# A two-layer hybrid decoder trunk on one core: norm factor broadcast a step later, first gate ahead of its mixing, recurrence gates moved around the output products, block products reordered

## The chip, the cores and the metric

The kernel runs on one core of a Trainium2 chip. The metric is device time in microseconds (us) of one execution; lower is better. A core has a matrix engine (TensorE, PE in the profile; PEld is its weight load), VectorE (DVE), ScalarE (ACT), GpSimd (POOL) and SyncE (SP), each working through its own list of instructions in order, and 16 DMA engines that all queues share. An instruction waits, where it has to, for a semaphore of another engine, and holds up everything behind it in its own list.

## The reference

Input x is 512 tokens by 1024 features; there are two layers. Cut to what matters here:

```python
for i in range(2):
    y = rms_norm(h, mix_norm[i])
    proj = y @ w_in[i]            # 1024 -> 6144, split into nine parts
    x_lru, g_lru, q, k, v, g_ret, u_sgu, v_sgu, g_sgu = split(proj)
    lru = rg_lru(causal_conv(x_lru), ...)            # 768 wide, 8 blocks of 96
    ret = retention(q, k, v, ...)                    # 6 heads of 128
    sgu = u_sgu * (w_s (per 128 tokens) @ layer_norm(v_sgu) + b_s)   # 512 wide
    mixed = concat(lru * silu(g_lru), ret * silu(g_ret), sgu * silu(g_sgu))
    h = h + mixed @ w_out[i]
    z = rms_norm(h, ple_norm[i])
    h = h + sigmoid(z @ w_ple_gate[i]) * (p[i] @ w_ple_proj[i])
return rms_norm(h, final_norm)
```

In rg_lru, two gates of each 96-wide block (sigmoids of small products) set the coefficients of a recurrence along the tokens: h[t] = a[t] h[t-1] + u[t].

## The kernel before, in words

**Number format.** A product is made in three matmuls (`mm3`, L212): every operand is split into a high part in a narrower format (`whi`, `y` with an even number) and the remainder (`wlo`, the odd number), and hi x hi, hi x lo and lo x hi are summed in PSUM. L214, L215 and L216 are these three.

**Weights.** `plan()` (L41) lists all weight chunks of 128 x 1024 in the order of their use. `prefetch` (L174) loads chunk i into a `raw` buffer (four of them) by SP's queue and converts it (`emit_cv`, L151): ACT casts it to `whi` (L165); the remainder is made by DVE (L170) or, for the chunks that L166 names, by ACT writing the negated copy into `wlo` (L167) and GpSimd's queue issuing a DMA that adds the chunk from memory to it (L168). `whi` and `wlo` have four buffers each, so a conversion waits until the chunk four places earlier has been used up on PE. In the first layer L166 names chunks 4 and 5, in the second all six chunks of x_lru (89 to 94 in the list).

**Order.** The code is written in steps (`step`, L192): prefetch up to four chunks ahead, the matmuls, then up to three pieces of background work from `bg` and one from `lazy`, then the evictions. The program's scheduler then merges these into a list for each engine, by its own estimates; the order within a list is fixed from then on.

**A layer.** It starts with six blocks of x_lru: a step of three blocks side by side (accumulators in three of the four PSUM banks `mm`), then three single ones. The norm's factor per token is wanted only after the products (the weights of the norm are folded into y, the factor is multiplied in at the evictions). `norm_stat` (L307) makes it: small matmuls `nst`, a chain of small DVE operations, and two diagonal matrices `nsgm` and `nsq`; `norm_bcast` (L335) spreads it over all partitions as `R` with two matmuls (`nR`, L337 and L338) and an ACT copy. The evictions of the blocks (`conv`, L545) multiply by `R` into `xs`; the taps `xcv` (L550, L552) follow and a DMA on ACT's queue puts the result into `U`.

Then come the products for v (four heads) and v_sgu as a 2 x 2 block product with seven products instead of eight (`FAST`, L30; `fast_step`, L590): W11, W21, Ta, Tc, Tb, Td, W22, each with two chunks and 24 matmuls. The sums of the y side are `uy` (L505 to L522, from ACT's `fz` and DVE's `fe`). The sums of the weight side are made in memory: W11's raw buffer `rawq` gets W12 added by a DMA of GpSimd's queue to become Ta, then W22 to become Tc, then W21 to become Td; each addition has to wait until the conversion before it has read the buffer. Tb is made of two blocks in a buffer of its own.

Next are four column blocks c of the spatial gate, each two steps of 24 matmuls: u with the mixing matmuls `mx` (L715) at its end, then the gate gs (`silu_scaled`); `fin` multiplies and splits into `sm`. The mixing needs the layer norm of v_sgu (`ln_apply`, ended by the four DVE operations of L635). Ahead of blocks 1 and 3 stand the gates of the recurrence groups 0 and 1 (`lru_group`, L645: four gate products of three matmuls each from `xc`, the split of U, then tanh, exp and square root on ACT and the recurrence on DVE, L689 to L693). `sgu_out` (L745) makes the part of the output product that belongs to the spatial gate, four steps f of 24 matmuls from `sm`, with group 2's gates ahead of f = 2; group 3's gates follow. Six heads of retention, the gates of the recurrence part, the rest of the output product and the per-layer embedding follow; the change leaves their order alone.

## Time and profile before

| | us |
|---|---|
| median of three runs | 933.3 |
| lowest and highest | 929.15, 934.02 |
| the profiled execution | 927.7 |
| its span, first to last instruction | 926.0 |
| mean granted TensorE clock (share of full speed) | 0.997 |

A row of the timeline has the start in us, the duration, engine, line and operation, what is written and read, and how many instructions were merged into the row; in brackets stands the idle time just before it and what ended it. Names in a row have their numbers left out. Matmuls overlap: one shows some 0.39 us, while the next begins 0.23 us after it. The profile names the releaser that came last by its events.

### The profile page before, as it was taken

Reading aid. Unit: us, or ns where it says so; the run is one execution under the profiler, and the core shown is the slowest. Engines: PE = TensorE matmul, PEld = TensorE weight load, DVE = VectorE, ACT = ScalarE, POOL = GpSimd, SP = SyncE. Lnnn points to the kernel's source line nnn. Section 1 sums busy time; section 2 is a strip of 40 time slices with the busy share of each in tenths; the row PEclk is TensorE's granted clock in tenths of the full one; section 3 lists DMA queues with packets and bytes.
Section 4 is the critical chain, followed back from the end, with each engine's and each line's share of the span. In section 5 each row is a group of like instructions: output and inputs, shape, how many; then the busy total and the mean of one; then the engine's idle time right before and its main releaser. Section 6 shows DMA issues by size and latency. Waiting matters only on the chain.

```text
span 926.0 us, 11714 instructions
## 1 busy us (share of the span) xinstructions
PE 901.6 (97%) x4354; PEld 748.7 (81%) x4354; DVE 659.7 (71%) x1281; ACT 460.5 (50%) x666; POOL 51.1 (6%) x52
## 2 busy tenths in 40 slices
PE   8999999999999999999989999999999999999997
PEld 7778787788888888888777778778889888888886
DVE  6979998987766754449529798789776676534564
ACT  6655678833233443335627438876333334334353
POOL 0210000000000000100311100000000000011020
PEclk9999999999999999999999999999999999999999
DMA  9968223232223433342558742232222323233302
GB/s 318 216 136 260 80 74 103 87 114 88 73 69 97 119 98 92 119 137 89 137 111 198 171 150 75 74 113 91 93 79 66 106 75 119 86 108 120 109 1 91
DMA packets 35177, 105.14 MB, mean 114 GB/s; under 512 B 4656, under 2 KB 5680, under 8 KB 35120
## 3 DMA queue, kind: packets, MB, share of 16 engines
q1 hardware_dynamic: 27248, 84.64, 28.3%
q0 software_dynamic: 3456, 12.58, 7.5%
q10 hardware_dynamic: 4416, 7.17, 2.6%
q8 instruction: 34, 0.56, 0.3%
q14 instruction: 23, 0.19, 0.1%
HBM read 95.99 MB, written 2.10 MB: 106 GB/s over the span
## 4 chain that ended last, share of the span: by engine, by line
PE 74%; DVE 9%; DMA 7%; ACT 5%; issue 4%; POOL 0%; ACTq 0%; DVEq 0%; POOLq 0%
PE acc L215 22%; PE acc L216 22%; PE acc L214 22%; DMA rawq<-in_wall 3%; DVE wlo L170 3%; DMA wlo<-in_wall 2%; DMA raw<-in_wall 2%; PE sc L824 1%; PE o L847 1%; DVE xcv L552 1%; ACT whi L165 1%; PE o L849 1%; PE kv L835 1%; PE pp L214 1%; DVE U L693 1%
## 5 line engine op out<-in xcount | busy, mean ns | idle before, releaser
L165 ACT CAST whi<-raw 128x1024 fp32r<-128x1024 f32 (+2 forms) x157 | 153.0, 978 | 303.2 <-PE acc L215 225.0
L214 PE MATMUL acc<-y,whi 128*128 128x512 f32 x608 | 242.0, 398 | 2.5 <-ACT whi L473 1.3
L216 PE MATMUL acc<-y,wlo 128*128 128x512 f32 x608 | 238.3, 392 | 3.9 <-DMA wlo<-in_wall 3.3
L215 PE MATMUL acc<-y,whi 128*128 128x512 f32 x608 | 237.8, 391 | 0.0
L170 DVE TENSOR_TENSOR wlo<-raw,whi 128x1024 fp32r<-128x1024 f32 (+2 forms) x149 | 167.4, 1125 | 75.2 <-ACT whi L165 75.0
L216 PEld LDWEIGHTS acc<-y,wlo 128*128 128x128 f32 x608 | 114.4, 188 | 30.0 <-DMA wlo<-in_wall 5.6
L214 PEld LDWEIGHTS acc<-y,whi 128*128 128x128 f32 x608 | 114.7, 189 | 25.9 <-ACT whi L473 1.6
L215 PEld LDWEIGHTS acc<-y,whi 128*128 128x128 f32 x608 | 114.8, 189 | 22.7
L305 POOL TENSOR_TENSOR nacc<-nacc,sq 128x512 f32<-128x512 f32 (+1 forms) x21 | 28.3, 1349 | 492.5 <-ACT sq L295 492.5
L214 PE MATMUL acc<-z,whi 128*128 128x512 f32 (+1 forms) x144 | 53.0, 368 | 0.0
L216 PE MATMUL acc<-z,wlo 128*128 128x512 f32 (+1 forms) x144 | 52.8, 366 | 0.0
L215 PE MATMUL acc<-z,whi 128*128 128x512 f32 (+1 forms) x144 | 52.7, 366 | 0.0
L214 PE MATMUL acc<-whi,y 128*128 128x256 f32 (+1 forms) x112 | 38.1, 341 | 1.2 <-ACT vs L615 1.2
L214 PE MATMUL acc<-ml,whi 128*128 128x512 f32 x96 | 37.3, 389 | 0.0
L215 PE MATMUL acc<-ml,whi 128*128 128x512 f32 x96 | 37.3, 389 | 0.0
L216 PE MATMUL acc<-rm,wlo 128*128 128x512 f32 x96 | 37.3, 389 | 0.0
L214 PE MATMUL acc<-rm,whi 128*128 128x512 f32 x96 | 37.3, 389 | 0.0
L216 PE MATMUL acc<-ml,wlo 128*128 128x512 f32 x96 | 37.3, 389 | 0.0
L215 PE MATMUL acc<-rm,whi 128*128 128x512 f32 x96 | 37.3, 389 | 0.0
L215 PE MATMUL acc<-wlo,y 128*128 128x256 f32 (+1 forms) x112 | 36.8, 329 | 0.0
L216 PE MATMUL acc<-whi,y 128*128 128x256 f32 (+1 forms) x112 | 36.8, 329 | 0.0
L912 DVE TENSOR_TENSOR hT<-hT,acc 128x512 f32<-128x512 f32 x16 | 11.0, 686 | 29.9 <-PE acc L216 29.9
(232 smaller groups left out, 1647.6 us busy)
## 6 DMA issues: line engine op xcount, KB each, us to landing
raw<-in_wall SPq DMA_DIRECT2D x119, 512.0 KB, 3.5
raw<-in_wall SPq DMA_DIRECT2D x32, 384.0 KB, 3.1
rawq<-in_wall POOLq DMA_DIRECT2D x12, 512.0 KB, 7.0
wlo<-in_wall POOLq DMA_DIRECT2D x8, 512.0 KB, 8.3
hT<-in_xT SPq DMA_DIRECT2D x8, 256.0 KB, 4.9
rawq<-in_wall SPq DMA_DIRECT2D x4, 512.0 KB, 5.9
raw<-in_wall POOLq DMA_DIRECT2D x4, 512.0 KB, 9.0
out_dram<-o SPq DMA_DIRECT2D x8, 256.0 KB, 2.1
```

The source lines that it names most:

```text
L165: SC.copy(hi[:m, :n], r[:m, :n])
L170: V.tensor_sub(lo[:m, :n], r[:m, :n], f32(hi[:m, :n]))
L214: T.matmul(out, wh, xh, start=first, stop=False, skip_group_check=more)
L215: T.matmul(out, wh, xl, start=False, stop=False, skip_group_check=more)
L216: T.matmul(out, wl, xh, start=False, stop=last, skip_group_check=more)
L305: (V if d == KD - 1 else e).tensor_add(nrm["acc"][:, c], nrm["acc"][:, c], sq[:, :n])
L552: V.scalar_tensor_tensor(u[:, j:], xs[:, : S - j], col(V_CW, l * 24 + 6 * (3 - j) + c), u[:, j:], op0=ALU.mult, op1=ALU.add)
L693: V.tensor_tensor_scan(u, A, u, 0.0, op0=ALU.mult, op1=ALU.add)
L824: T.matmul(b[:, n, :], k[:, c], q[:, c], start=True, stop=True)
L835: T.matmul(kv[:, n, :], hd["kn"][:, n, :], values(h, n), start=True, stop=True)
L847: T.matmul(o[:, c], hd["s"][:, n, :], values(h, n), start=True, stop=n == 0)
L912: V.tensor_add(hT[:, d, :], hT[:, d, :], accs[j])
```

## The change

1. `FAST`: Ta stands second, ahead of W21 (the plan of chunks follows).
2. `plan()`: in the first column block the gate gs stands ahead of u, and `osg`, the chunks of `sgu_out`, follow group 2's gate weights; the loop over c and `sgu_out` follow: group 2's gates stand ahead of `sgu_out`, and the splits of U for groups 1, 2 and 3 are queued one step later, after the gate step, and in step f = 0.
3. L166: chunks 89, 90 and 91 (the first three of x_lru in the second layer) get their remainder from DVE, no longer from ACT and a DMA.
4. The first half of the first three chunks is loaded by SP's queue, in turn with the pieces of x, no longer by ACT's queue.
5. The evictions of the first three blocks of x_lru are held back until block 3 has been multiplied, `norm_stat` stays with the step of three, and `norm_bcast` comes after block 3; blocks 4 and 5 take their accumulators from the two banks `sc`.
6. `fin` of the first column block is queued by u's eviction.

```diff
--- before.py
+++ after.py
@@ -27,7 +27,7 @@
 LRU_GROUPS = [(0, 1), (2, 3), (4, 5), (6, 7)]
 
 
-FAST = (("W11", "x11", "X"), ("W21", "x12", "Z"), ("Ta", "u1", "Y"), ("Tc", "v2", "X"), ("Tb", "v3", "X"), ("Td", "x22", "X"), ("W22", "u4", "Y"))
+FAST = (("W11", "x11", "X"), ("Ta", "u1", "Y"), ("W21", "x12", "Z"), ("Tc", "v2", "X"), ("Tb", "v3", "X"), ("Td", "x22", "X"), ("W22", "u4", "Y"))
 FIRST = ("W11", "W21", "Ta")
 RSQRT_MAGIC = 1597463007.0
 ROUND = 12582912.0
@@ -48,8 +48,8 @@
         for c in range(4):
             if c % 2 == 1:
                 out += [lg[c // 2]]
-            out += [(l, "in", OFF["u"] + P * c, 1024), (l, "in", OFF["gs"] + P * c, 1024)]
-        out += [(l, "osg", 0, 1024), (l, "osg", 1, 1024), lg[2], (l, "osg", 2, 1024), (l, "osg", 3, 1024), lg[3]]
+            out += [(l, "in", OFF[n] + P * c, 1024) for n in (("u", "gs") if c else ("gs", "u"))]
+        out += [lg[2]] + [(l, "osg", f, 1024) for f in range(4)] + [lg[3]]
         for h in range(NH):
             if h == 4:
                 out += [(l, "inv", (OFF["v"] + P * h, kh), 1024) for kh in range(2)]
@@ -163,7 +163,7 @@
             lo = wp.tile([P, 1024], F32R, tag="wlo", name=f"wlo{i}")
             m = rows(chunks[i])
             SC.copy(hi[:m, :n], r[:m, :n])
-            if kind == "in" and idx < OFF["gl"] and i > 3:
+            if kind == "in" and 3 * P <= idx < OFF["gl"] and i > 3:
                 SC.activation(lo[:m, :n], r[:m, :n], AF.Copy, scale=-1.0)
                 G.dma_start(out=lo[:m, :n], in_=source(chunks[i]), accum_op=ALU.add)
             else:
@@ -229,12 +229,11 @@
 
     first3 = [wp.tile([P, 1024], F32, tag="raw", name=f"raw{i}") for i in range(3)]
     half = [slice(0, 512), slice(512, 1024)]
-    for i in range(3):
-        nc.scalar.dma_start(out=first3[i][:, half[0]], in_=source(chunks[i])[:, half[0]])
     for d in range(KD):
         nc.sync.dma_start(out=hT[:, d, :], in_=a["xT"][:, d, :])
-        if 3 <= d < 6:
-            nc.sync.dma_start(out=first3[d - 3][:, half[1]], in_=source(chunks[d - 3])[:, half[1]])
+        if d < 6:
+            i, h = d % 3, half[d // 3]
+            nc.sync.dma_start(out=first3[i][:, h], in_=source(chunks[i])[:, h])
     st.update(raw=3, cv=3)
     spt = tp.tile([P, S], F32, tag="r0", name="spt")
     lam, *sp_tmp = [spt[:, 2 * NB * i : 2 * NB * i + 2 * NB] for i in range(5)]
@@ -344,14 +343,14 @@
         nrm["rn"] = rn
 
 
-    def feat_steps(l, y, kinds, evicts, look=LOOK, n_bg=3, mid=None, n_lazy=1):
+    def feat_steps(l, y, kinds, evicts, look=LOOK, n_bg=3, mid=None, n_lazy=1, tag=()):
 
         accs = []
 
         def pe():
             ws = [take(l, *k) for k in kinds]
             for _ in kinds:
-                accs.append(bank())
+                accs.append(bank(*tag))
             for k in range(KD):
                 for acc, (wh, wl) in zip(accs, ws):
                     mm3(acc, wh[:, P * k : P * k + P], wl[:, P * k : P * k + P], *y[k], k == 0, k == KD - 1)
@@ -559,12 +558,14 @@
 
             return f
 
-        feat_steps(l, y, [("in", P * c) for c in range(3)], [conv(c) for c in range(3)], mid=norm_finish, n_lazy=0)
+        held = []
+        feat_steps(l, y, [("in", P * c) for c in range(3)], [held.append] * 3, mid=norm_stat, n_lazy=0)
         bg.extend([f for j in range(4) for f in fast_sums(j)])
         if l == 0:
             lazy.appendleft(softplus)
-        for c in range(3, 6):
-            feat_steps(l, y, [("in", P * c)], [conv(c)], n_lazy=0)
+        feat_steps(l, y, [("in", P * 3)], [lambda acc: [conv(c)(x) for c, x in enumerate(held + [acc])]], mid=norm_bcast, n_lazy=0)
+        for c in range(4, 6):
+            feat_steps(l, y, [("in", P * c)], [conv(c)], n_lazy=0, tag=("sc", 2))
         rn = nrm["rn"]
 
 
@@ -720,37 +721,37 @@
                 V.tensor_mul(m1, m1, nrm["R"])
                 hold["m1"] = m1
 
+            def fin(c=c, hold=hold):
+                V.tensor_mul(hold["m2"], hold["m2"], hold["sg"])
+                split_to(sm[c], hold["m2"])
+
             def u_ev(acc):
                 hold["m2"] = tp.tile([P, S], F32, tag="m2", name=f"m2_{c}")
                 V.tensor_mul(hold["m2"], hold["m1"], acc)
+                if c == 0:
+                    bg.append(fin)
 
             def g_ev(acc):
-                sg = silu_scaled(acc, f"s{c}")
-                m2 = hold["m2"]
-
-                def fin(c=c):
-                    V.tensor_mul(m2, m2, sg)
-                    split_to(sm[c], m2)
-
-                bg.append(fin)
+                hold["sg"] = silu_scaled(acc, f"s{c}")
+                if c:
+                    bg.append(fin)
 
             if c % 2 == 1:
                 drain()
                 lru_group(c // 2)
+            if c == 0:
+                feat_steps(l, y, [("in", OFF["gs"])], [g_ev])
+                bg.append(lru_split(0))
             feat_steps(l, y, [("in", OFF["u"] + P * c)], [u_ev], mid=mix)
-            if c % 2 == 0:
-                bg.append(lru_split(c // 2))
-            feat_steps(l, y, [("in", OFF["gs"] + P * c)], [g_ev])
+            if c > 1:
+                bg.append(lru_split(c - 1))
+            if c:
+                feat_steps(l, y, [("in", OFF["gs"] + P * c)], [g_ev])
 
         def sgu_out():
             for f in range(4):
                 accs = []
-                if f == 1:
-                    bg.append(lru_split(2))
-                elif f == 2:
-                    drain()
-                    lru_group(2)
-                elif f == 3:
+                if f == 0:
                     bg.append(lru_split(3))
 
                 def pe():
@@ -771,6 +772,7 @@
 
 
         drain()
+        lru_group(2)
         sgu_out()
         drain()
         lru_group(3)
```

On PE, in the first layer, the two matmuls of the norm's broadcast stood before in the middle of block 3 (weights `whi3`, `wlo3`):

```order
L216 MATMUL acc_384<-y0_6_128,wlo3_226 128x512
L214 MATMUL acc_384<-y0_8_130,whi3_225 128x512
L215 MATMUL acc_384<-y0_9_131,whi3_225 128x512
L337 MATMUL nR_337<-nsgm_327,onesr_106 128x512
L216 MATMUL acc_384<-y0_8_130,wlo3_226 128x512
L214 MATMUL acc_384<-y0_10_132,whi3_225 128x512
L215 MATMUL acc_384<-y0_11_133,whi3_225 128x512
L338 MATMUL nR_337<-nsq_328,onesr_106 128x512
L216 MATMUL acc_384<-y0_10_132,wlo3_226 128x512
```

and stand now between block 3 and block 4 (`whi4`, `wlo4`, whose remainder is one that a DMA makes):

```order
L214 MATMUL acc_371<-y0_14_136,whi3_225 128x512
L215 MATMUL acc_371<-y0_15_137,whi3_225 128x512
L216 MATMUL acc_371<-y0_14_136,wlo3_226 128x512
L336 MATMUL nR_396<-nsgm_327,onesr_106 128x512
L337 MATMUL nR_396<-nsq_328,onesr_106 128x512
L214 MATMUL acc_429<-y0_0_122,whi4_355 128x512
L215 MATMUL acc_429<-y0_1_123,whi4_355 128x512
L216 MATMUL acc_429<-y0_0_122,wlo4_356 128x512
```

They moved ten matmuls further back. The lists of the second layer show the same.

On PE, in the first layer, the last gate step of the spatial gate (`acc_1331`) was followed by the output products from `sm0`:

```order
L214 MATMUL acc_1331<-y0_14_136,whi29_1188 128x512
L215 MATMUL acc_1331<-y0_15_137,whi29_1188 128x512
L216 MATMUL acc_1331<-y0_14_136,wlo29_1189 128x512
L214 MATMUL acc_1375<-sm0_0_903,whi30_1234 128x512
L215 MATMUL acc_1375<-sm0_1_904,whi30_1234 128x512
L216 MATMUL acc_1375<-sm0_0_903,wlo30_1235 128x512
L214 MATMUL acc_1375<-sm0_2_905,whi30_1234 128x512
```

and is followed now by group 2's gate products, from `xc02` (`xc02_0` and `xc02_2` are written by ACT, `xc02_1` and `xc02_3` by DVE), taken in between the first output products:

```order
L214 MATMUL acc_1390<-xc02_0_1361,whi30_1234 96x512
L214 MATMUL acc_1398<-xc02_2_1363,whi30_1234 96x512
L214 MATMUL acc_1408<-xc02_2_1363,whi30_1234 96x512
L214 MATMUL acc_1421<-sm0_0_903,whi31_1270 128x512
L215 MATMUL acc_1421<-sm0_1_904,whi31_1270 128x512
L216 MATMUL acc_1421<-sm0_0_903,wlo31_1271 128x512
L214 MATMUL acc_1421<-sm0_2_905,whi31_1270 128x512
L215 MATMUL acc_1421<-sm0_3_906,whi31_1270 128x512
L216 MATMUL acc_1421<-sm0_2_905,wlo31_1271 128x512
L214 MATMUL acc_1421<-sm0_4_907,whi31_1270 128x512
L215 MATMUL acc_1421<-sm0_5_908,whi31_1270 128x512
L215 MATMUL acc_1383<-xc02_1_1362,whi30_1234 96x512
```

The twelve gate matmuls moved ahead of the 48 output matmuls of f = 0 and f = 1, some of which now stand between them.

On DVE at the same place, the last block's product `m2_3` and its split `sm0_7` stood ahead of `xc02`:

```order
L693 SCALAR_TENSOR_TENSOR U_196<-rg02_1243,U_196 96x512
L692 TENSOR_TENSOR U_196<-U_196,lT3_1309 96x512
L732 TENSOR_TENSOR m2_3_1323<-m2_3_1323,sxs3_1363 128x512
L693 SCALAR_TENSOR_TENSOR U_196<-rg03_1258,U_196 96x512
L170 TENSOR_TENSOR wlo33_1372<-raw33_1268,whi33_1371 128x1024
L385 TENSOR_TENSOR sm0_7_910<-m2_3_1323,sm0_6_909 128x512
L497 TENSOR_TENSOR xc02_1_1437<-U_196,xc02_0_1436 96x512
L497 TENSOR_TENSOR xc02_3_1439<-U_196,xc02_2_1438 96x512
```

and stand now behind it (`lT`, `rg` and `U` are group 1's recurrence, `L693` before and `L694` now the scan):

```order
L694 SCALAR_TENSOR_TENSOR U_196<-rg02_1243,U_196 96x512
L693 TENSOR_TENSOR U_196<-U_196,lT3_1309 96x512
L496 TENSOR_TENSOR xc02_1_1362<-U_196,xc02_0_1361 96x512
L694 SCALAR_TENSOR_TENSOR U_196<-rg03_1258,U_196 96x512
L496 TENSOR_TENSOR xc02_3_1364<-U_196,xc02_2_1363 96x512
L725 TENSOR_TENSOR m2_3_1323<-m2_3_1323,sxs3_1371 128x512
L170 TENSOR_TENSOR wlo33_1380<-raw33_1268,whi33_1379 128x1024
L384 TENSOR_TENSOR sm0_7_910<-m2_3_1323,sm0_6_909 128x512
```

On ACT, in the second layer, the cast of Ta's first chunk (`whi99`) stood behind the sums for the y side:

```order
L384 CAST uy1_10_4028<-fe21_4177 128x512
L511 ACTIVATE fz30_4178<-hT_73,vec_71 128x512
L511 ACTIVATE fz31_4179<-hT_73,vec_71 128x512
L609 COPY v1_0_4341<-acc_4352 128x512
L165 CAST whi99_4393<-rawq95_4182 128x1024
L384 CAST uy1_12_4030<-fe30_4180 128x512
L609 COPY v1_1_4342<-acc_4353 128x512
L384 CAST uy1_14_4032<-fe31_4181 128x512
```

and now Ta's chunk is `whi97`, cast ahead of most of them:

```order
L165 CAST whi97_4287<-rawq95_4168 128x1024
L383 CAST uy1_4_4019<-fe10_4158 128x512
L510 ACTIVATE fz20_4160<-hT_73,vec_71 128x512
L383 CAST uy1_6_4021<-fe11_4159 128x512
L510 ACTIVATE fz21_4161<-hT_73,vec_71 128x512
L549 ACTIVATE xcv1_4426<-xs1_1_4032,vec_71 128x512
L549 ACTIVATE xcv2_4473<-xs1_2_4033,vec_71 128x512
L549 ACTIVATE xcv3_4516<-xs1_3_4034,vec_71 128x512
L383 CAST uy1_8_4023<-fe20_4162 128x512
L383 CAST uy1_10_4025<-fe21_4163 128x512
L510 ACTIVATE fz30_4164<-hT_73,vec_71 128x512
L510 ACTIVATE fz31_4165<-hT_73,vec_71 128x512
```

`whi97` stands now ahead of eleven other instructions, among them the sums `fz` and `uy` of three of the four quarters; `whi98` follows behind them.

## The prediction

> **What bounds the kernel now.** I read the page's busy times first, then PE's waits, then the rows around the largest of them.
>
> ```profile
> PE 901.6 (97%) x4354; PEld 748.7 (81%) x4354; DVE 659.7 (71%) x1281; ACT 460.5 (50%) x666; POOL 51.1 (6%) x52
> ...
> DVE  6979998987766754449529798789776676534564
> ```
>
> PE is busy for 901.6 of 926.0 us, so the whole change can only win from the 24 us in which PE stands still. DVE matters by place: slices 3 to 5 of 40 (69 to 139 us) and some later ones are 90% full or more. PE's waits by what ended them (total, times, longest):
>
> ```profile
> PE acc L216 <- DMA wlo<-in_wall: 3.3, 3, 2.6
> PE acc L215 <- DVE wlo L170: 2.4, 4, 0.8
> PE mx L715 <- DVE vs L635: 1.8, 2, 0.9
> PE nR L337 <- DVE nsgm L332: 1.7, 2, 1.4
> ...
> PE acc L215 <- DVE xc L497: 1.3, 4, 0.3
> ...
> PE acc L214 <- ACT vs L615: 1.2, 1, 1.2
> ...
> PE acc L216 <- DVE pg L953: 0.6, 1, 0.6
> PE acc L215 <- DVE sm L385: 0.6, 2, 0.3
> PE acc L214 <- ACT sm L384: 0.5, 2, 0.3
> PE acc L214 <- ACT whi L165: 0.4, 1, 0.4
> ```
>
> These ten rows are 13.8 us, and every edit aims at some of them. A wait costs more than its bracket, because matmuls overlap:
>
> ```profile
> 141.95 0.39 PE L216 MATMUL acc<-y,wlo 128*128 128x512 f32 x1
> 142.18 0.39 PE L214 MATMUL acc<-sm,whi 128*128 128x512 f32 x1
> ```
>
> One shows 0.39 but the next starts after 0.23, so a stall loses its bracket plus 0.39 - 0.23 = 0.16. I call this the addition. Gains below are in us, with the ends I allow in brackets.
>
> **Broadcast a step later: 0 [-0.8, 2.0].**
>
> ```profile
> 31.95 0.47 PE L337 MATMUL nR<-nsgm,onesr 128*128 128x512 f32 x1 [1.42 <-DVE nsgm L332]
> 35.88 0.50 PE L216 MATMUL acc<-y,wlo 128*128 128x512 f32 x1 [0.38 <-DMA wlo<-in_wall]
> 488.10 0.50 PE L216 MATMUL acc<-y,wlo 128*128 128x512 f32 x1 [0.31 <-DMA wlo<-in_wall]
> ```
>
> ```profile
> 27.19 8.64 DMA wlo<-in_wall
> ```
>
> The two waits at `nR`, 1.7 in the table above with two additions, are 2.0 together and vanish: ten matmuls (2.3) now run first. But block 4's remainder is made by a DMA that starts at 27.19 and lands at 35.83, tied to ACT and GpSimd, not to PE's wait. PE would reach 35.88's matmul some 2 us sooner and stand there until the same moment. The second layer shows the same wait at 488.10, behind a transfer from the same place of the code. So I take nothing. The upper end is a transfer that starts earlier by as much; the lower is the held evictions (three blocks' accumulators stay some 5 us longer) stopping blocks 4 and 5 once per layer for 0.4.
>
> **Remainders of the second layer's first chunks by DVE: +3.5 [2.5, 3.5].**
>
> ```profile
> 467.27 0.50 PE L216 MATMUL acc<-y,wlo 128*128 128x512 f32 x1 [2.58 <-DMA wlo<-in_wall]
> ```
>
> ```profile
> 458.36 0.69 DVE L951 TENSOR_TENSOR pg<-acc,R 128x512 f32<-128x512 f32 x1 [1.51 <-PE acc L216]
> ```
>
> ```profile
> 458.13 1.05 ACT L165 CAST whi<-raw 128x1024 fp32r<-128x1024 f32 x1 [1.54 <-PE acc L215]
> ```
>
> In the same step a matmul of the same form waits 0.6, put down to `pg` in the table, which it doesn't read; its weight is a remainder made by a DMA too. Together they lose 0.6 + 2.6 + 2 x 0.16 = 3.5. Done on DVE, the third remainder is ready 1.2 us after the cast that ends at 459.18 (a subtraction's time is in the row of two at 507.49 below), at 460.4, seven us before the matmul that waited. DVE has time: it had just idled 1.51. On DVE three subtractions more, 3.6 us, then stand among the evictions that end the layer before; should they delay `pg` and through it the layer's end by 1, the lower end holds.
>
> **Block products reordered: +2.6 [0.3, 5.0].** The waits of W21 and Ta for remainders go: 2.4, the first `v_sgu` copy's 1.2 and the cast's 0.4, with six additions of 0.16 make 5.0. A new one comes in the second layer. Ta's first chunk is a memory sum in `rawq`:
>
> ```profile
> DMA to landing us min/median/max: 10.9/10.9/10.9
> ```
>
> ```profile
> 486.31 0.86 POOL L145 DMA_DIRECT2D rawq<-in_wall x1 [0.65 <-DVE kf L814]
> ```
>
> ```profile
> 488.04 1.51 ACT L550 ACTIVATE xcv<-xs,vec 128x512 f32<-128x512 f32 x2
> ...
> 498.63 1.05 ACT L165 CAST whi<-raw 128x1024 fp32r<-128x1024 f32 x1 [2.11 <-PE acc L215]
> 499.59 1.13 ACT L384 CAST uy<-fe 128x512 fp32r<-128x512 f32 x2
> 500.63 1.34 ACT L511 ACTIVATE fz<-hT,vec 128x512 f32<-128x512 f32 x2
> ```
>
> ```profile
> 507.49 2.35 DVE L170 TENSOR_TENSOR wlo<-rawq,whi 128x1024 fp32r<-128x1024 f32 x2
> ```
>
> ```profile
> 506.59 0.39 PE L215 MATMUL acc<-wlo,y 128*128 128x512 f32 x1
> ```
>
> The sum lands at 486.31 + 10.9 = 497.2. ACT's list has its cast early, so ACT stands until then with `fz` and `uy` behind it. From there to the last `uy` that Ta's second half needs are 2 casts of chunks (0.95 each, start to start), 5 `uy` (0.52), 4 `fz` (0.62), 3 `xcv` (0.70) and a copy (0.5): 9.6, so 506.8. Then DVE makes its `uy` (0.6, as the sum at 146.52 below) and the remainder `wlo98` (1.1): 508.5. PE wants that remainder at the place where 506.59 stands now, the second product's second half, and waits 1.9. In the first layer ACT's copies fall behind the issue of the taps' DMAs; I put 0.5 there, about one cast's half. 5.0 - 1.9 - 0.5 = 2.6. The upper end is neither wait; the lower doubles both, 5.0 - 4.8 = 0.2, say 0.3.
>
> **First gate ahead of its mixing: +2.1 [-0.5, 2.1].** The mixing matmuls' two waits, 1.8 + 2 x 0.16, go: 16 matmuls (3.6) in the first layer and 20 (4.5) in the second now run first, against waits of 0.9. What hides `vs` is then the gate's 24 matmuls; its weights are ready by the same prefetch. `fin` moves a step back, and `sm0` isn't read before the output products, 35 us on. Lower end: u's eviction a quarter us late in each layer.
>
> **Group 2's gates ahead of the output products: -2.3 [-5.0, 3.7].** The waits at `sm` (0.6, 0.5) and `xc` (1.3) go, 2.4 + 8 x 0.16 = 3.7. What replaces them is at the end of the gate step, at 142.18 in the row above:
>
> ```profile
> 142.32 1.34 ACT L684 ACTIVATE sT<-lT,cst 96x512 f32<-96x512 f32 x2
> 143.57 0.50 ACT L165 CAST whi<-raw 96x384 fp32r<-96x384 f32 x1
> 144.09 1.28 ACT L391 ACT_TABLE_LOAD   x1
> 145.38 0.63 ACT L391 ACTIVATE sxs<-sxs 128x512 f32<-128x512 f32 x1
> ...
> 146.86 0.61 ACT L496 CAST xc<-U 96x512 fp32r<-96x512 f32 x1
> ```
>
> ```profile
> 145.38 1.21 DVE L693 TENSOR_TENSOR_SCAN U<-rg,U 96x512 f32<-96x512 f32 x1
> 146.52 0.66 DVE L692 TENSOR_TENSOR U<-U,lT 96x512 f32<-96x512 f32 x1
> ```
>
> In the new list ACT has group 1's square roots `sT`, the gates' weight `whi30`, then the casts `xc02`. By these rows the weight is cast at 144.07, `xc02_0` half a us later, at 144.6: PE, which wants it at 142.18, waits 2.5. `xc02_2` is there at 145.15; twelve matmuls from the first start PE arrives at `xc02_1` near 147.5, which DVE can make only behind the second sum at 146.52 and has at 147.74 (0.25 late), and `xc02_3` behind one more scan (1.14) at 149.5 (0.3 late). That is 3.0, taken for both layers: 3.7 - 6.0 = -2.3. Upper end: none of it. Lower: `xc` or `sm` late once more in each, 1.35. Group 3's gates stay without a wait by little: 96 output and 12 gate matmuls (24.5) and the 3.0 of waits bring PE there 27.5 us after 142.18, and I estimate from the lists, where its split now stands in step f = 0, that it is ready 0.3 sooner.
>
> The new order puts two more table loads on ACT in the first layer, one to `cos` and one back. The row at 144.09 is one: 1.28 and the next activation starts as it ends, so I put 1.3 each, in ACT's idle half. [...]
>
> **Prologue by SP's queue: +0.8 [0, 2.8].**
>
> ```profile
> 8.59 0.79 PE L214 MATMUL acc<-y,whi 128*128 128x512 f32 x1 [1.28 <-ACT whi L473]
> ...
> 10.46 0.63 PE L214 MATMUL acc<-y,whi 128*128 128x512 f32 x1
> 10.88 0.63 PE L215 MATMUL acc<-y,whi 128*128 128x512 f32 x1
> ```
>
> ```profile
> 9.00:10.00 1.00, 1.00 (x3) 0.74 (x3) 1.00 (x2) 0.16 (x1) 0.00 (x0) 0.50 1.05 404
> ```
>
> The second matmul waits 1.28 for the second half-chunk, which comes by another queue than x; with both in order of use that wait and its addition, 1.44, should go. But the granted clock there is 0.50 (eighth column), the DMA engines full (1.05), and matmuls come 0.42 apart. 1.44 buys 1.44 / 0.42 = 3.4 matmuls by the time the clock rises, worth 3.4 x 0.23 = 0.8. If the clock is full from the start, 1.44 and seven matmuls at 0.2 each, 2.8; if the transfers are the limit, 0. [...]
>
> **Sum.** 0 + 3.5 + 2.6 + 2.1 - 2.3 + 0.8 = 6.7. The profiled execution, 927.7 (span 926.0), would become 921.0. It is 5.6 below the median of the runs, 933.3; put on that, the forecast is 926.6. Half a per cent, 4.7 us, is about what a measurement of this kernel can tell from no change: faster means below 928.6, slower above 938.0.
>
> **Rivals.**
> *Group 2's operands are early.* If ACT and DVE reach `xc02` 2.5 us sooner than the rows add up to (upstream waits that go give PE no lead, say), no new wait stands there: 6.7 + 6.0 = 12.7, 920.6. For it: DVE and ACT lose work ahead (`m2_3`, `sm0_7` moved behind). Against: ACT's `sT` starts only at 142.32, after the time PE asks. Chance 0.16.
> *DVE is the bound in the first layer.* Where it is 90% full, a PE that comes sooner only waits later at the next remainder. Then the gains of the first layer go again: the prologue's 0.8, the block products' 1.5 there and the mixing's 1.1. 6.7 - 3.4 = 3.3, 930.0. For: the digits of DVE's row, and 8.4 of the 13.8 us of waits listed end at DVE. Against: its waits there were at single late results, not at every remainder. Chance 0.18.
> *Ta's memory sum is late in both layers.* If the first layer's takes 10.9 like the second's, PE stands 3.5 more: 3.2, 930.1. Against it, the other DMA sums of that place took 8.6. Chance 0.04.
> [...]
> *Slower: PE held in its list at group 2's first gate.* Before, output products from a finished `sm0` lay between the last gate step and group 2 and covered any lateness of ACT and DVE; now nothing does. Each us by which `sT`, the weight's cast or `xc02_0` are later than reckoned is paid by PE in full, in both layers: time = 926.6 + 2x. It is slower than 938.0 from x = 5.7; at x = 6, 938.6. For: DVE is full there. Against: that is more than the whole chain of rows from 142.32 to 144.6. Chance 0.06.
> *The broadcast's edit doesn't do what it says* is inside the forecast, as its 0.
>
> **How the numbers follow.** Forecast 0.54, with 923.3 to 928.6 as its own range (gains of 10 to 4.7). It and the early operands are faster, 0.70; DVE as bound, Ta's sum and the table switches are within half a per cent, 0.24; the held PE is slower, 0.06. The range reaches below to the early operands with the prologue's clock granted sooner by 0.8, 919.8, and above to DVE as bound with the broadcast's -0.8 and half of group 2's wait in one layer again, 1.5: 930.0 + 2.3 = 932.3. Some 0.05 lie below, 0.15 above.
>
> **What would show it.** Right: no wait at `nR`, and one of about 2 at the `wlo` that a DMA makes, in both layers, behind it; none of over 0.3 between 458 and 466; none at `mx`; in the second layer a wait of 1 to 3 in Ta's second half for DVE's `wlo`; in both a wait of some 2.5 for ACT's `xc` or its weight at the first gate product after the gate step; the second matmul without its 1.28. Wrong: waits there of under 1 or above 4, a wait at the remainders of the first layer's block products as long as those removed, or a PE whose brackets sum to over 24 us.

## The result, and the profile after

| us | before | after |
|---|---|---|
| median of 12 runs each | 933.0 | 923.4 |
| lowest and highest | 925.1, 935.0 | 921.3, 926.9 |
| profiled execution's span | 926.0 | 920.9 |
| its mean granted clock | 0.997 | 0.995 |

The ratio of the new times to the old is 0.9917, with a 95% interval of 0.9895 to 0.994: faster by 0.8%. The forecast was 926.6, within 919.8 to 932.3, and faster with a chance of 0.7. The profiled spans differ by 5.1, forecast 6.7; the medians differ by 9.6, more than either, and that is one of the things to explain.

The page's busy times after the change, then PE's waits:

```profile
PE 900.2 (98%) x4354; PEld 752.0 (82%) x4354; DVE 663.6 (72%) x1284; ACT 459.8 (50%) x665; POOL 48.8 (5%) x49
```

```profile
PE acc L214 <- ACT xc L495: 5.1, 2, 2.8
PE acc L216 <- DMA wlo<-in_wall: 4.6, 2, 2.5
...
PE mx L716 <- DVE vs L636: 1.0, 1, 1.0
PE acc L215 <- DVE wlo L170: 0.7, 1, 0.7
PE acc L215 <- DVE xc L496: 0.7, 1, 0.7
PE acc L214 <- ACT vs L614: 0.2, 1, 0.2
```

Many small waits became four large ones. `nR`, `sm` and `pg` are gone from the list; `xc` on ACT is new, and the remainders by DMA cost more than before (4.6 against 3.3). The rows, in order of time:

```profile
33.32 0.50 PE L216 MATMUL acc<-y,wlo 128*128 128x512 f32 x1 [2.10 <-DMA wlo<-in_wall]
100.51 0.46 PE L716 MATMUL mx<-ws,vs 128*128 128x128 f32 x2 [1.01 <-DVE vs L636]
142.06 0.47 PE L214 MATMUL acc<-xc,whi 96*96 96x512 f32 x1 [2.83 <-ACT xc L495]
485.46 0.50 PE L216 MATMUL acc<-y,wlo 128*128 128x512 f32 x1 [2.48 <-DMA wlo<-in_wall]
504.77 0.51 PE L215 MATMUL acc<-wlo,uy 128*128 128x512 f32 x1 [0.66 <-DVE wlo L170]
591.28 0.47 PE L214 MATMUL acc<-xc,whi 96*96 96x512 f32 x1 [2.30 <-ACT xc L495]
```

Four stretches of the same kernel (PE, PEld, DVE, ACT and POOL busy, then the granted clock as eighth column, DMA share, GB/s): the prologue, and the time just behind three of those rows.

```profile
10.00:11.00 1.00, 1.00 (x5) 0.82 (x5) 0.90 (x3) 0.80 (x2) 0.00 (x0) 1.00 1.05 406
34.00:35.00 1.00, 1.00 (x4) 0.81 (x3) 1.00 (x3) 0.30 (x1) 1.00 (x2) 0.50 1.07 234
145.00:146.00 1.00, 1.00 (x3) 0.74 (x3) 1.00 (x2) 1.00 (x2) 0.00 (x0) 0.50 0.65 254
592.00:593.00 1.00, 1.00 (x5) 0.80 (x5) 1.00 (x2) 1.00 (x1) 0.00 (x0) 1.00 0.00 0
```

Behind the waits of 2.10 and 2.83 PE runs at half clock for 3.4 us: eight matmuls 0.43 apart and not 0.23, 1.6 us lost, with PE shown as fully busy. Behind 2.30 and 2.48 in the second layer the clock stays. The prologue is the opposite: no half clock any more.

Behind which wait the clock halves can be read from the granted clock in the profiles. Its stretches at 0.50 (the run's last one apart) last 3.41 us, or twice that, and within a run they start on one grid of 3.41 us: here at 33.98 and 143.21, 32 steps apart, in the first profile of the kernel before at 8.21 and 922.99, 268 steps apart. What sets the waits with half clock behind them apart is how long PE stands idle within one cell of the grid. These are the four cells that hold most of each wait, and the cell behind the third; the number behind a cell's length is PE's busy time:

```profile
30.57:33.98 3.41, 1.30 (x6) 0.76 (x5) 3.38 (x9) 1.67 (x3) 1.45 (x3) 1.00 1.05 274
139.80:143.21 3.41, 1.15 (x5) 0.76 (x6) 3.40 (x6) 3.39 (x6) 0.00 (x0) 1.00 0.03 7
481.13:484.54 3.41, 1.85 (x9) 1.17 (x7) 3.37 (x12) 2.15 (x3) 1.25 (x2) 1.00 1.00 245
484.54:487.95 3.41, 2.49 (x11) 2.08 (x12) 3.41 (x8) 2.75 (x5) 0.00 (x0) 1.00 1.06 219
586.94:590.36 3.42, 2.04 (x10) 1.34 (x8) 3.05 (x7) 3.39 (x5) 0.00 (x0) 1.00 0.02 7
```

PE is idle for 2.1 us of the first cell and 2.3 of the second, and the next cell runs at half clock. The grid cuts the 2.48 into 1.57 and 0.92 and the 2.30 into 1.38 and 0.92, and the clock stays. In the fourteen profiles of this document, between PE's first and last matmul, all 21 cells with 1.97 us or more of such idle time are followed by a cell at half clock, 4 of the 12 with 1.57 to 1.86 are, and none of the 221 with less. In the profiles of before and after alone the three cells with 2.11, 2.12 and 2.26 are followed by half clock, and the next two by length, with 1.67 and 1.57, are not.

To place gains, the PE matmul with the same count in both kernels is compared, after less before; negative is earlier:

| up to | after - before | of it here | forecast |
|---|---|---|---|
| prologue (matmul 50) | -2.5 | -2.5 | -0.8 |
| first six blocks, layer 1 (150) | -0.95 | +1.6 | 0 |
| block products (300) | -3.3 | -2.3 | -1.5 |
| gate and mixing (450) | -3.1 | +0.2 | -1.05 |
| group 2's first gates (600) | +0.4 | +3.5 | +1.15, this row and the next |
| group 3 (750) | -0.3 | -0.7 | |
| start of layer 2 (2200) | -4.2 | -3.9 | -3.5 |
| its other blocks (2250) | -2.6 | +1.5 | 0 |
| its block products (2450) | -5.4 | -2.75 | -1.1 |
| gate and mixing (2550) | -6.6 | -1.2 | -1.05 |
| group 2 (2750) | -3.8 | +2.8 | +1.15, this row and the next |
| group 3 (2850), and to the end | -5.1 | -1.3 | |

Group 2's four rows sum to +4.3, where the forecast had +2.3.

### The profile page after: what moved, and what is told of

It is laid out like the page before. It is cut to its first block, busy times and chain, and to the rows that moved or that the text cites. A ratio compares the mean times of both kernels' runs of the same rounds, so it can differ in the third digit from the quotient of the medians.

```text
span 920.9 us, 11714 instructions
## 1 busy us (share of the span) xinstructions
PE 900.2 (98%) x4354; PEld 752.0 (82%) x4354; DVE 663.6 (72%) x1284; ACT 459.8 (50%) x665; POOL 48.8 (5%) x49
## 4 chain that ended last, share of the span: by engine, by line
PE 82%; DVE 9%; DMA 3%; issue 3%; ACT 2%; SPq 0%; DVEq 0%; POOL 0%; ACTq 0%; POOLq 0%
PE acc L216 24%; PE acc L215 24%; PE acc L214 24%; DVE wlo L170 2%; DMA rawq<-in_wall 1%; PE sc L826 1%; PE o L849 1%; DMA wlo<-in_wall 1%; PE o L851 1%; PE kv L837 1%; PE pp L214 1%; DVE xcv L551 1%; PE pp L216 1%; PE pp L215 1%; DVE rope L415 1%
## 5 line engine op out<-in xcount | busy, mean ns | idle before, releaser
L170 DVE TENSOR_TENSOR wlo<-raw,whi 128x1024 fp32r<-128x1024 f32 (+2 forms) x152 | 171.2, 1129 | 75.5 <-ACT whi L165 75.4
```

The costliest lines, as they stand in the source:

```text
L170: V.tensor_sub(lo[:m, :n], r[:m, :n], f32(hi[:m, :n]))
```

## The experiments

Theory A, mine: each wait of PE adds where it stands, so the parts can be undone one by one; the broadcast's gain is taken back by the next remainder by DMA. Theory B, the rival in each case: DVE, ACT or something else sets the pace and PE only meets it elsewhere. Twelve kernels were run; each is compared with runs of the kernel before on the same chip, and the ratios are to it. A wait "above pace" is its bracket plus the 0.16 by which matmuls overlap.

### Group 2's gates back between the output products

```diff
-        out += [lg[2]] + [(l, "osg", f, 1024) for f in range(4)] + [lg[3]]
+        out += [(l, "osg", 0, 1024), (l, "osg", 1, 1024), lg[2], (l, "osg", 2, 1024), (l, "osg", 3, 1024), lg[3]]
...
-            if c > 1:
-                bg.append(lru_split(c - 1))
+            if c == 2:
+                bg.append(lru_split(1))
...
-                if f == 0:
+                if f == 1:
+                    bg.append(lru_split(2))
+                elif f == 2:
+                    drain()
+                    lru_group(2)
+                elif f == 3:
                     bg.append(lru_split(3))
...
-        lru_group(2)
         sgu_out()
```

> The changed kernel with group 2's gates and the splits of U for groups 2 and 3 back where they stood, between the output products of f = 1 and f = 2. Theory A (each wait of PE adds to the time where it stands): the stretch from the last gate step to the end of group 3 lost 8.4 us above pace in the changed kernel's two layers (4.5 + 0.4 + 3.5, of it 1.6 at half clock), and 4.2 in the kernel before; its span falls by 4.2, from 920.9 to 916.7, and the ratio to the kernel before from 0.9917 to about 0.987. Theory B (ACT and DVE are what is late, and PE meets their lateness at some other place instead): the waits at group 2 go and others of the same size come, span 920 to 922.

Measured: span 916.3, median 918.1, ratio 0.9866 (0.9841 to 0.9891). Theory A to within half a us: by the count of matmuls 4.0 of the 4.5 came off at group 2's places, and the rest is what differences of up to 3.1 each way leave, at places that this edit doesn't touch. (In the changed kernel the splits of U for groups 2 and 3 are queued earlier than before, not later, and group 1's is where it was; the edit puts those two back.) The old waits at `sm` and `xc` returned, 2.6 us of brackets against 5.8 at `xc`. So the move, as made, costs about 0.5%; it is the one part shown to make the kernel slower. PE still met something new in the second layer's block products:

```profile
500.19 0.50 PE L215 MATMUL acc<-wlo,uy 128*128 128x512 f32 x1 [2.23 <-DVE wlo L170]
```

This is the wait at Ta's second half that the forecast put at 1.9. In the changed kernel's own profile it was 0.66, and not because the memory sum was faster: it took 10.97 us there and 10.49 here, and in both this matmul starts 11.64 after the sum has landed. PE itself came later there. It had stood 2.48 at the remainder of chunk 93 (block 4's in the second layer) shortly before, here 0.45. In the five kernels with the late broadcast, the new block order and remainders by DMA the two waits together are 2.7 to 3.3: what the first takes, the second doesn't.

### Filling the wait

The kernel after, with ten matmuls in each layer ahead of group 2's gates whose result is not used:

```diff
+            if g == 2:
+                fill = bank("o", 1, name="fill")
+                for _ in range(10):
+                    T.matmul(fill, onesr, sm[0][0], start=True, stop=True)
             for b in grp:
```

> The changed kernel with ten matmuls of 128x512 whose result nobody reads put on PE in front of group 2's first gate product in each layer, where it stood idle 2.8 and 2.5 us; they take 2.3. Theory A (PE's standing still is what halves the granted clock after it): the wait itself stays, the matmuls behind it in the first layer start 0.23 apart and not 0.43, span 919.4 (1.5 less), the second layer as before. Theory B (the clock falls for another cause, such as load on the chip at that time): the stretch at half clock stays, span 920.9 or more.

```profile
139.89 2.50 PE L674 MATMUL fill<-sm,onesr 128*128 128x512 f32 x10
142.89 1.23 PE L214 MATMUL acc<-xc,whi 96*96 96x512 f32 x4 [0.51 <-ACT xc L495]
```

```profile
143.00:144.00 1.00, 1.00 (x5) 0.60 (x6) 1.00 (x2) 0.98 (x2) 0.00 (x0) 1.00 0.00 0
145.00:146.00 1.00, 0.96 (x5) 0.46 (x3) 1.00 (x2) 1.00 (x2) 0.00 (x0) 1.00 0.94 287
```

The gates come no sooner, but the clock is 1.00 where it was 0.50. In the six other profiles that have this wait in the first layer, of 2.3 to 2.9, the clock halved behind it each time. So what halves it there is PE standing still. The whole didn't gain: span 922.1, median 923.7, ratio 0.9924 (0.9897 to 0.9951). In this profile two other waits, of 2.8 at block 4's remainder and 2.3 at Ta's, had half clock behind them.

### The kernel before once more

> The kernel before once more, unchanged, for the span and the granted clock of each of its runs: its profiled run of 927.7 with a clock of 0.997 lies 3 to 5 below its medians of 931 to 933. Theory A (its usual runs hold stretches at half clock behind its longest stalls, each 1.6, which the profiled one did not): runs of 930 and more have clocks of 0.990 to 0.995, and the time falls as the clock rises, some 1.6 per 0.002. Theory B (the usual runs have longer waits for transfers, with a full clock): clocks of 0.996 and more in runs of 930 and more.

The profiled run's span was 930.6, at 0.994. PE's first row of waits and its largest wait, which was 2.58 in the first profile:

```profile
PE acc L216 <- DMA wlo<-in_wall: 7.5, 4, 4.1
```

```profile
469.11 0.80 PE L216 MATMUL acc<-y,wlo 128*128 128x512 f32 x1 [4.06 <-DMA wlo<-in_wall]
```

```profile
470.00:471.00 1.00, 1.00 (x4) 0.71 (x4) 0.00 (x0) 0.00 (x0) 0.00 (x0) 0.50 0.91 184
```

Both causes are there. Theory A's sign came: nine of the 12 runs took 930 or more, all at clocks of 0.990 to 0.995, and none at the 0.996 that theory B asked for. But the DMAs that make remainders also land later, as theory B had it (3.3 us of waits in the first profile, 7.5 here), and behind the longest wait the clock halves. Over its 12 runs the spans go from 926.1 at a clock of 0.997 to 933.2 at 0.993 and 933.0 at 0.990; over the changed kernel's 12, from 919.6 at 0.997 to 925.2 at 0.989. One half-clock stretch of 3.4 us lowers the mean clock by 0.0018 and costs 1.6, so the clock alone explains about half of those 7 us at 0.993 and most of them at 0.990. So the profile on which the forecast was built is near the best that the kernel before has, and the change, which took three of its DMA remainders away, is worth more in its usual runs than there (9.6 between the medians, 5.1 between the profiles).

### Three remainders by DVE, alone

```diff
-            if kind == "in" and idx < OFF["gl"] and i > 3:
+            if kind == "in" and idx < OFF["gl"] and i > 3 and not 89 <= i <= 91:
```

> The kernel before with one edit only: the remainders of chunks 89, 90 and 91 by DVE. Theory A (what the layer's start gains, the next remainder by transfer takes in part): the waits of 0.6 and 2.6 near 461 and 467 go (3.7 with the additions) and the wait for chunk 92's remainder near 485 grows from 0.3 to some 2; span 924, 2 below 926.0, and a ratio that can hardly be told from 1. Theory B (the term as forecast, 3.5 with nothing behind it): span 922.5 and the wait for chunk 92 stays at 0.3.

Median 926.4, ratio 0.994 (0.992 to 0.9959), span 921.5: 4.5 below 926.0, of it 3.8 at the place of the three chunks. Waits for remainders by DMA in all:

```profile
PE acc L216 <- DMA wlo<-in_wall: 1.1, 1, 1.1
```

That one is block 4's in the first layer. Block 4's in the second layer, near 485 (it is chunk 93; my theory calls it 92), had none here, though 2.48 in the changed kernel. My theory, that it grows as the layer's start gains, fell: its transfer took 6.7 us here, 9.0 in the changed kernel, 7.5 and 9.4 in the two profiles of the kernel before. Made alone, this part gives 0.6%, where the whole change gives 0.8%.

### All remainders by DVE

```diff
-            if kind == "in" and 3 * P <= idx < OFF["gl"] and i > 3:
+            if kind == "in" and idx < 0:
```

> The changed kernel with every remainder made by DVE, none by ACT and a transfer: chunks 4 and 5 and the second layer's 92, 93 and 94 too. Theory A (the transfers give the broadcast's gain back): the waits of 2.3 and 2.6 for them go, and the half clock of 1.4 behind the first; span 914.6, ratio about 0.985. Theory B (DVE is the bound, the transfers are there because it has no time): five more subtractions of 1.2 us come out of DVE's full stretches, PE waits for other remainders or taps, span 919 to 923.

Span 915.2, median 918.4, ratio 0.9868 (0.9842 to 0.9895). Theory A. From PE's waits:

```profile
PE acc L214 <- ACT xc L495: 5.0, 2, 2.7
...
PE nR L336 <- DVE nsgm L331: 1.1, 1, 1.1
```

No wait for a remainder is left anywhere; DVE's five subtractions more (6 us) came out of time that PE didn't need, but for the 1.1 at `nR` in the first layer. DVE is 90% busy in much of that layer, and the two subtractions more there cost PE little else.

### The broadcast: alone, undone, and undone with DVE's remainders

Alone on the kernel before (point 5 of the change and nothing else, with the new argument `tag` of `feat_steps`):

```diff
-        feat_steps(l, y, [("in", P * c) for c in range(3)], [conv(c) for c in range(3)], mid=norm_finish, n_lazy=0)
+        held = []
+        feat_steps(l, y, [("in", P * c) for c in range(3)], [held.append] * 3, mid=norm_stat, n_lazy=0)
...
-        for c in range(3, 6):
-            feat_steps(l, y, [("in", P * c)], [conv(c)], n_lazy=0)
+        feat_steps(l, y, [("in", P * 3)], [lambda acc: [conv(c)(x) for c, x in enumerate(held + [acc])]], mid=norm_bcast, n_lazy=0)
+        for c in range(4, 6):
+            feat_steps(l, y, [("in", P * c)], [conv(c)], n_lazy=0, tag=("sc", 2))
```

> The kernel before with one edit only: the norm's broadcast a step later (evictions held, blocks 4 and 5 in the other two banks). Theory A (the transfer of the next remainder sets when PE goes on, as forecast: 0): the waits at nR (1.6 and 0.5) vanish, those for the remainders of the blocks behind them grow to 2.1 to 2.9 in the first layer and by 0.5 in the second, and the longer one may have a stretch at half clock behind it; ratio 0.999 to 1.002. Theory B (the edit is worth its waits and more, since it also reorders the taps): ratio 0.994 to 0.997.

```profile
36.20 0.50 PE L216 MATMUL acc<-y,wlo 128*128 128x512 f32 x1 [2.75 <-DMA wlo<-in_wall]
```

```profile
77.81 0.55 PE L214 MATMUL acc<-whi,uy 128*128 128x512 f32 x1 [2.35 <-ACT vs L615]
```

Median 934.4, ratio 1.0018 (0.9994 to 1.0041): no gain, perhaps a loss. The waits at `nR` went, and the remainder's took their sum; new was 2.35 at ACT's copy of `vs`.

In the first layer the waits at `nR` and at block 4's remainder add up to the same for the same transfer, wherever the broadcast stands. Eleven profiles have that remainder by DMA. From PE's matmul 112, ahead of `nR` in all of them, to matmul 130, the third of block 4, PE loses the transfer's time less 6.3 us against a pace of 0.227 per matmul, five times with the early broadcast and six times with the late one:

| profile | broadcast | transfer, us | PE's loss, us |
|---|---|---|---|
| before | early | 8.64 | 2.33 |
| three remainders by DVE | early | 9.31 | 2.99 |
| group 2's gates back | late | 7.99 | 1.67 |
| prologue undone | late | 8.64 | 2.33 |
| filled wait | late | 9.27 | 2.96 |

The other six fit as well. At chunk 93, block 4's in the second layer, the loss is again the transfer's time less 6.3 in ten of the eleven; in the eleventh (three remainders by DVE) the transfer took 6.7 and landed 0.4 before PE came. That is the forecast's "given back". What it missed is that one wait of 2.1 to 2.8 is worse than two of 1.4 and 0.4: in the first layer the clock halved behind the single one in five of the six profiles (not behind 1.48), behind the split ones in none of the five.

Undone on the changed kernel:

```diff
-        feat_steps(l, y, [("in", P * c) for c in range(3)], [held.append] * 3, mid=norm_stat, n_lazy=0)
+        feat_steps(l, y, [("in", P * c) for c in range(3)], [conv(c) for c in range(3)], mid=lambda: (norm_stat(), norm_bcast()), n_lazy=0)
...
-        feat_steps(l, y, [("in", P * 3)], [lambda acc: [conv(c)(x) for c, x in enumerate(held + [acc])]], mid=norm_bcast, n_lazy=0)
-        for c in range(4, 6):
-            feat_steps(l, y, [("in", P * c)], [conv(c)], n_lazy=0, tag=("sc", 2))
+        for c in range(3, 6):
+            feat_steps(l, y, [("in", P * c)], [conv(c)], n_lazy=0)
```

> The changed kernel with the norm's broadcast, the evictions and the accumulators of the first six blocks as they were before. Theory A: the waits at nR return (1.6 and 0.5), those for the remainder by DMA shrink to what they were (0.55 and 0.5), and no stretch at half clock follows them; the six blocks' loss falls from 6.6 to 3.3, span 917.6, ratio about 0.988. Theory B (the edit itself is worth its 2.0 us, and the long waits come from something else in the change, such as the earlier start): the waits at nR return on top of the long ones, span 922 to 923, ratio 0.993 to 0.994.

Span 922.5, median 926.0, ratio 0.994 (0.992 to 0.996); the interval overlaps the changed kernel's. Neither theory: the remainder's waits stayed at 1.72 and 2.35 with 0.24 and 0.31 at `nR`, as if given back, and the first six blocks came out 1.4 sooner, with no half clock behind the 1.72. But the kernel lost elsewhere. In the second layer's block products PE waits 1.66 and smaller sums for ACT's copies of `vs`, which the changed kernel doesn't show. The block order alone, below, has the same wait of 1.66, also with the early broadcast. So the early broadcast and the new block order don't go together in these two kernels.

The same edit on the kernel with all remainders by DVE:

> The changed kernel with all remainders by DVE and the norm's broadcast back where it was. Theory A (with no transfer behind it the later broadcast does pay): waits at nR of 1.6 to 2.7 and 0.5 to 0.7 where the kernel with the late broadcast and DVE's remainders had 1.2 and none; and the second layer's block products wait for ACT's copies of vs some 2 to 3, as in the two kernels with the early broadcast and the new block order; span 3 to 5 above that kernel's 915.2, 918 to 920, ratio 0.990 to 0.992. Theory B (where the broadcast stands makes no difference): span 914 to 916.5, ratio 0.986 to 0.988.

```profile
32.98 0.47 PE L336 MATMUL nR<-nsgm,onesr 128*128 128x512 f32 x1 [1.34 <-DVE nsgm L331]
35.93 0.50 PE L214 MATMUL acc<-y,whi 128*128 128x512 f32 x1 [1.40 <-DVE xs L556]
...
483.73 0.50 PE L214 MATMUL acc<-y,whi 128*128 128x512 f32 x1 [1.50 <-DVE xs L556]
```

Span 918.5, 3.3 above 915.2, as theory A had it, but by other waits. The scheduler left `nR` behind block 3 (matmul 126 of PE's list, as in the changed kernel; in the run before this one it was back at 116), so this run doesn't try the early broadcast, and the 2 to 3 at the copies of `vs` didn't come (0.5). What costs is that block 4 waits in both layers for the evictions `xs` to free a bank. Between these two profiles the held evictions and the two other banks are worth 3 us. The timings, 0.9872 (0.9843 to 0.99) against 0.9868, don't show such a difference, so that worth is open.

### The block order alone

```diff
-FAST = (("W11", "x11", "X"), ("W21", "x12", "Z"), ("Ta", "u1", "Y"), ("Tc", "v2", "X"), ("Tb", "v3", "X"), ("Td", "x22", "X"), ("W22", "u4", "Y"))
+FAST = (("W11", "x11", "X"), ("Ta", "u1", "Y"), ("W21", "x12", "Z"), ("Tc", "v2", "X"), ("Tb", "v3", "X"), ("Td", "x22", "X"), ("W22", "u4", "Y"))
```

> The kernel before with one edit only: Ta ahead of W21. Theory A (the forecast's term: 5.0 of waits go, 0.5 to 2.4 come): waits of W21 and Ta for remainders go, as does the 1.2 at the copy of vs; in the second layer a wait of 0.5 to 2.2 at Ta's remainder, which hangs on the memory sum of some 11 us; span 921 to 923.5. Theory B (DVE and ACT are as late as before, PE meets it at another block product): 925 to 927.

Median 931.3, ratio 0.9989 (0.9969 to 1.0008), span 927.8. The first layer gains 2.1 over this place; the second loses 1.7. ACT's rows there (ACTq is its queue issuing DMAs), and PE's:

```profile
521.37 2.03 ACTq L554 DMA_DIRECT2D U<-xcv  x2
526.47 0.81 ACT L550 ACTIVATE xcv<-xs,vec 128x512 f32<-128x512 f32 x1 [2.44 <-DMA U<-xcv]
527.19 1.03 ACT L165 CAST whi<-rawq 128x1024 fp32r<-128x1024 f32 x1
528.12 0.57 ACT L613 COPY vs<-acc 128x512 f32<-128x512 f32 x1
```

```profile
528.75 0.50 PE L214 MATMUL acc<-whi,uy 128*128 128x512 f32 x1 [1.66 <-ACT vs L613]
```

The copy that frees PE's bank stands on ACT behind a cast and a tap `xcv`, and the tap waits 2.44 until the DMA of an earlier tap, issued from ACT's own list at 521.37, is through. The forecast saw the copies behind the taps' DMAs and gave that 0.5 in the first layer; it is 1.66 here, in the second. In the changed kernel, with the late broadcast, it is 0.2 in the first layer and nothing in the second. So in these runs this part pays only beside the other. The reason is read from the lists and not tried.

### Prologue, and gate ahead of mixing, undone

```diff
+    for i in range(3):
+        nc.scalar.dma_start(out=first3[i][:, half[0]], in_=source(chunks[i])[:, half[0]])
     for d in range(KD):
...
-        if d < 6:
-            i, h = d % 3, half[d // 3]
-            nc.sync.dma_start(out=first3[i][:, h], in_=source(chunks[i])[:, h])
+        if 3 <= d < 6:
+            nc.sync.dma_start(out=first3[d - 3][:, half[1]], in_=source(chunks[d - 3])[:, half[1]])
```

> The changed kernel with the first half-chunks on ACT's queue as before. Theory A (what the start gains stays to the end): the second matmul waits 1.3 to 1.8 again, six or seven matmuls run at half clock, span 2.5 above 920.9, 923.4, ratio about 0.9945. Theory B (block 4's remainder by transfer takes it back): the wait there shrinks by as much, span 920.5 to 921.5, ratio as the changed kernel's.

```profile
8.23 0.75 PE L214 MATMUL acc<-y,whi 128*128 128x512 f32 x1 [1.23 <-ACT whi L473]
```

```profile
9.00:10.00 1.00, 1.00 (x3) 0.78 (x3) 0.70 (x2) 0.00 (x0) 0.00 (x0) 0.50 1.04 402
```

Matmul 50 comes 2.3 later, span 923.7, median 925.9, ratio 0.9931 (0.9904 to 0.9958): theory A by the profile; the times alone don't separate it from the changed kernel's. (The half clock of the prologue is back; chunk 93's remainder and Ta's took 0.50 and 2.27, where the changed kernel had 2.48 and 0.66.)

```diff
-            out += [(l, "in", OFF[n] + P * c, 1024) for n in (("u", "gs") if c else ("gs", "u"))]
+            out += [(l, "in", OFF[n] + P * c, 1024) for n in ("u", "gs")]
```

> The changed kernel with u and its mixing ahead of the gate in the first column block, as before. Theory A (in the first layer DVE reaches vs late whatever stands first, so the edit pays in the second layer alone): the first layer's wait at mx is about 1 to 1.3 above pace as with the gate first, the second layer's of 1.1 returns; span 1 above 920.9, 922, ratio 0.992 to 0.994. Theory B (each of the two waits was cut): the first layer's wait at mx rises to 2 or more; span 923, ratio 0.994 to 0.995.

```profile
PE mx L716 <- DVE vs L636: 1.6, 2, 1.3
```

Ratio 0.9923 (0.9899 to 0.9946), span 924.0, of which most lies at other places, in the prologue and behind waits that this edit doesn't touch. At `mx` PE waits 1.3 and 0.3 with u first, 1.0 and none with the gate first: 0.6 for both layers. That is theory A in its direction, with 0.3 in the second layer where it had 1.1. But the edit doesn't bring the old order back on PE: in the first layer the scheduler puts the mixing at matmul 409 with either order (393 in the kernel before), in the second at 2495 (2506 with the gate first, 2486 before).

### Both corrections together

All remainders by DVE and group 2's gates back, the edits of the two sections above:

```diff
-            if kind == "in" and 3 * P <= idx < OFF["gl"] and i > 3:
+            if kind == "in" and idx < 0:
...
-        lru_group(2)
         sgu_out()
```

> The changed kernel with group 2's gates back between the output products, and all remainders by DVE. Theory A (the terms add up): 4.6 and 5.7 below the changed kernel's span of 920.9, 910.6, give or take 2 for a stretch at half clock that comes or goes; ratio to the kernel before about 0.980. Theory B (the gains overlap, since what one gives the next wait takes): 914 to 916, no better than one of them alone, ratio 0.985 to 0.987.

```profile
PE acc L215 <- DVE xc L496: 1.3, 4, 0.3
...
PE acc L214 <- ACT vs L614: 0.9, 1, 0.9
PE mx L716 <- DVE vs L636: 0.9, 1, 0.9
PE nR L336 <- DVE nsgm L331: 0.9, 1, 0.9
```

```profile
core 0: 911.7 us, clock 0.999
```

Median 913.6, ratio 0.9796 (0.9769 to 0.9822): 2% below the kernel before and 1.2 points below the changed one. The terms add up (910.6 forecast, 911.7 measured). No single wait of PE above 1.2 is left, none halves the clock behind it, and its four runs lie within 1.3 us.

## Why the prediction was right, point by point

- **Remainders by DVE, +3.5:** right in the profile (3.9 at that place). As a kernel of its own it is worth more, 4.5 between profiles and 5.3 between medians; the longer waits for those transfers in the second profile of the kernel before point to the reason. That goes far to answer the difference between the medians: the forecast carried a gain worked out in a good run over to the median unchanged.
- **Broadcast, 0:** the mechanism is shown. The forecast named the place (a wait of about 2 behind it at the remainder by DMA), and PE's loss there follows the transfer's time alone. The 1.5 lost in the second layer isn't the edit's: that transfer took 9.0 us where it had been 7.5, and over the kernels, with either broadcast, 6.7 to 9.5. The half clock behind the single long wait, 1.6 in the first layer, was in no term. And the forecast didn't see that the block order pays only beside the late broadcast.
- **Block products, +2.6:** mis-sized: 5.05 in the changed kernel (2.3 and 2.75), its upper case. The wait at Ta stands where it was foretold but was 0.66, where 1.9 was worked out and the prediction's own signs asked for 1 to 3; in three other kernels it was 2.2 to 2.3. The forecast's way to it was right: it has the matmul's operand 11.3 us behind the memory sum, and the matmul came 11.64 behind. But PE had just stood 2.48 at chunk 93 and met less of it. The copies of `vs`, priced at 0.5 in the first layer, cost 0.2. And the part is no gain of its own: alone it gives nothing that can be told, since those copies then cost 1.66 in the second layer.
- **Gate ahead of the mixing, +2.1:** half right. The second layer's wait went (1.2 there); the first layer's is still 1.01. The step that failed is "16 matmuls (3.6) in the first layer ... now run first, against waits of 0.9": the mixing stands those 16 matmuls further back, but DVE's list has 3.8 us more work ahead of `vs` (three taps, a remainder and some smaller operations more). `vs` starts 25.3 us behind PE's 300th matmul, before 21.5, and DVE has no idle moment between the two in either kernel. So the first mixing matmul starts at 100.51, and before it started at 100.00, though PE is 3.3 us ahead at the 300th matmul. The rival "DVE is the bound in the first layer" is right at this one place; it would have taken the prologue's and the block products' gains as well, and those stayed.
- **Group 2's gates, -2.3:** the sign and the wait are right: 2.83 and 2.30 where 2.5 was worked out from ACT's list, and the small ones at `xc` behind it 0.7 where 0.55 was. The term is short by 2.0, of which 1.6 is the half clock behind the first wait.
- **Prologue, +0.8:** mis-sized. Nearly the upper case, 2.8, came (2.5, and 2.3 when it was undone): without the two gaps ahead of it the clock was 1.00 from the second matmul, at 6.84, on. No run shows the 0.8 by which the forecast's low end, 919.8, has the clock granted sooner; what the runs showed in its place is that full clock, within the 2.5. The kernel before can also keep its clock there. In its first profile 2.1 us of two gaps fell into one cell of the clock's grid, and the clock halved; in the profile with three remainders by DVE gaps of 1.3 and 1.2 fell into two cells, and it didn't.
- **Half clock:** the forecast gave it to the prologue alone. In these profiles it stands behind a cell of the grid of 3.41 us in which PE is idle for long enough: 1.97 us always were, and less than 1.57 never. Of the 27 waits of 2.1 to 2.9 us 17 had half clock behind them; the 2.58 of the first profile had not, since the grid cut it into 1.67 and 0.91. Where the grid falls differs from profile to profile (one of its steps lies at 1.38 us of the first profile's span, at 3.26 of the changed kernel's), so that part is chance.
- **Table switches:** the two added loads took 1.28 each, and the next activation began as each ended, as the forecast's 1.3 each has it. Switches at twice that price, for which 0.02 of the forecast's 0.24 stands, are shown by no run. ACT's rows in the kernel after:

```profile
150.24 1.28 ACT L432 ACT_TABLE_LOAD   x1
151.53 0.72 ACT L432 ACTIVATE cosT<-rope,cst 128x512 f32<-128x512 f32 x1
152.28 1.28 ACT L663 ACT_TABLE_LOAD   x1
153.57 0.68 ACT L663 ACTIVATE rg<-acc,vec 96x512 f32<-96x512 f32 x1
```

The misses nearly cancel: prologue +1.7, block products +2.4, remainders +0.4; broadcast -3.1, group 2 -2.0, mixing -1.1. Together -1.7, from 6.7 to the 5.1 measured between the profiles, but for rounding. The single terms miss by 10.7 us in all, so that the sum came this close is in good part luck; the broadcast's -1.5 in the second layer is a long transfer, and it made the block products' +2.4 in part, since a PE that stands longer at chunk 93 waits less at Ta. The median, 923.4, lies 3.2 below the forecast for the reason given first: the profile behind the forecast was a good run.

## What to carry to other kernels

When a wait is removed, look for the next transfer that PE meets whose start doesn't depend on that wait: only what is left of it there is gained. Gather many waits into one and the sum may be the same while the cost is higher: here 1.97 us or more of idle time within one 3.41 us cell of the clock's grid had half clock in the next cell each time. And before an edit is undone to see its worth, compare the engines' lists: the scheduler may leave the instructions where they were. Last, ask of the profile from which a forecast is made whether it is a usual run: its mean clock and its longest DMA waits, beside a few other runs, tell.
